# Eight seven-product slots instead of six in the second half of a feed-forward down product

## The chip, the cores and the metric

The kernel runs on one core of a Trainium2 chip. TensorE (PE) multiplies, VectorE (DVE) and ScalarE (ACT) do the elementwise work, GpSimd (POOL) almost nothing, and SyncE (SP) issues nearly all the DMAs. The metric is the device time of one execution in microseconds; the kernel before takes 1433.44 us (median of three runs, 1433.04 to 1433.55).

## The reference

One decoder block over 256 tokens of width 2048, in float32. Two attention branches are gated, merged and added to the input; then comes a feed-forward part, and a last norm over each token:

```python
h2 = rmsnorm(x, ffn_norm_w[l])
up = causal_dwconv(h2 @ w_ffn_up[l], conv_w[l], conv_b[l])
a, b = jnp.split(up, 2, axis=-1)
x = x + (jax.nn.silu(a) * b) @ w_ffn_down[l]      # 256 x 5632 times 5632 x 2048
return rmsnorm(x, final_norm_w)
```

The change touches only the product with `w_ffn_down`.

## The kernel before, in words

**Split products.** Each float32 operand is kept as a high part (rounded to the type that PE multiplies in one pass) and a low part (the rest). A product of 128x128 by 128x512 is three matmuls: high by high, high by low, low by high (`mm3`). ACT makes the high part of a weight tile by a copy (L161), DVE the low part by a subtraction (L162).

**The weight stream.** Weights come from HBM in tiles of 128x1024 called raw (512 KB, `load`, L144), always four in flight or in use (`RAW_BUFS`). `part(n)` splits tile n into whi and wlo, of which there are four each, and only then asks for tile n + 4, which takes the place of one that has been read. SP issues the loads in program order, and each waits there until its place is free.

**The down product in slots.** The 2048 output columns are four groups of 512, taken as two pairs (p = 0 and 1). The 5632 rows are 22 pieces of 256. A slot is one piece against one pair of groups: two raw tiles, two blocks of 128 tokens, two of 128 rows, two of 512 columns. As eight block products this is 24 matmuls (a plain slot). `down()` lists 22 slots for each pair; the last four of the second pair are regrouped so that column group 3 is finished first. What runs in slot q + 1 is prepared while PE works on slot q.

**Seven-product slots.** In the slots that the table `SEVEN` names, the 2x2x2 block product is done with seven block products instead of eight, so 21 matmuls, by sums of blocks on both sides. The weight side's sums are made in `seven_parts` (L685 to L698): five ACT copies and nine DVE operations over the two raw tiles, in place; L687 and L698 are 128x1024 wide, the other seven DVE operations 128x512. Its results go to whi and wlo, and to the single tiles called t (t14 and t2). The last two DVE operations (L697, L698) are also the last readers of the two raw tiles. The last products of the seven use L698's result. The token side's sums, called s, are made once for each piece by `seven_sums`: one DVE operation of 128x512 and four of 128x128 in a scratch tile called room (L717 to L721), then a high and low split. They are made in the first pair and used again in the second. Four extra sums of products, e0 to e3, collect in the accumulators that the other pair of columns does not need at that time; `gathered` adds them to x2 after the last seven-product slot, in two steps of four DVE operations.

**Between and after the pairs.** After the first pair, `added` adds the first two column groups to x2 (DVE, L786) and, a slot later, takes squares for the final norm (ACT, L790, which writes into the same accumulators). In the second pair `wf`, the weights of the final norm, is loaded into the places of one set of s and of room (L829); `weighted` multiplies them in (L795), and `finish` ends one block of 128 tokens at a time (L541 to L560).

**What sets the order.** There is no scheduler: each engine runs its instructions in program order, which is the order in which `down_slots` writes them in each slot: first the preparation of the next slot, then the sums, then one step of each task that was spawned (`run_tasks`), then the products.

Of the kernel before, what the change touches and what calls it, by code (L numbers as in the profile page):

```python
# [10 lines left out]
F32R = mybir.dt.float32r  # L11
# [6 lines left out]
P = 128  # L18
# [60 lines left out]

SEVEN = ((4, 7, 10, 13, 16, 18), (3, 5, 8, 10, 13, 15))


def down():

    out = []
    for p, where in enumerate(SEVEN):
        c = 2 * p
        rest = list(range(len(where), NFB // 4 * 2))  # L90
        for i in range(NFB // 2):
            if p == 1 and i == NFB // 2 - 4:
                for d in (c, c + 1):
                    out += [(False, [(rest[j], d), (rest[j + 1], d)]) for j in (0, 2)]
                break
            k = where.index(i) if i in where else rest.pop(0)
            out.append((i in where, [(k, c), (k, c + 1)]))
    return out
# [3 lines left out]
def block(ctx: ExitStack, tc: tile.TileContext, a):  # L102
# [8 lines left out]
    px = ctx.enter_context(tc.tile_pool(name="px", bufs=1))  # L111
# [6 lines left out]
    def f32(ap):  # L118
        return ap.bitcast(F32)
# [38 lines left out]
    def split2(hi, lo, full, scale=None):  # L158

        if scale is None:  # L160
            nc.scalar.activation(hi, full, AF.Copy)  # L161
            nc.vector.tensor_sub(lo, full, f32(hi))  # L162
        else:
            nc.scalar.activation(hi, full, AF.Copy, scale=scale)
            nc.vector.scalar_tensor_tensor(lo, full, scale, f32(hi), op0=OP.mult, op1=OP.subtract)
# [6 lines left out]
    def mm3(out, ah, al, bh, bl, start, stop, **kw):  # L172
        mm(out, ah, bh, start=start, stop=False, **kw)
        mm(out, ah, bl, start=False, stop=False, **kw)
        mm(out, al, bh, start=False, stop=stop, **kw)
# [71 lines left out]
    xb = [xtiles[k // 2][:, k % 2] for k in range(KD)]  # L247
# [7 lines left out]
    big = {}  # L255
# [447 lines left out]
    def two_blocks(k):  # L703

        f = 2 * k
        if f < 16:
            x = "rm"[f // 8]
            return ot[x + "h"][:, f % 8:f % 8 + 2, :], ot[x + "l"][:, f % 8:f % 8 + 2, :]
        return big["gh"][:, f - 16:f - 14, :], big["gl"][:, f - 16:f - 14, :]

    def seven_sums(k):


        ah, al = two_blocks(k)
        room = big["room"]
        x, sums = room[:, 0, :].rearrange("p (k t) -> p k t", k=2), room[:, 1, :].rearrange("p (i t) -> p i t", i=4)
        nc.vector.tensor_add(x, f32(ah), f32(al))  # L717
        nc.vector.tensor_add(sums[:, 0, :], x[:, 0, P:], x[:, 1, P:])
        nc.vector.tensor_sub(sums[:, 2, :], x[:, 0, :P], x[:, 0, P:])
        nc.vector.tensor_sub(sums[:, 1, :], sums[:, 0, :], x[:, 0, :P])  # L720
        nc.vector.tensor_sub(sums[:, 3, :], x[:, 1, :P], sums[:, 1, :])  # L721
        pool_k, tag = (px, f"xb{k}") if k < 5 else (big["pf"], "wa")
        big["s", k] = pool_k.tile([P, 2, 4, P], F32R, name=f"s{k}", tag=tag, bufs=1)
        split2(big["s", k][:, 0], big["s", k][:, 1], sums)

    def seven_products(k, accs, extra, halves):

        xs = two_blocks(k)
        sums = big["s", k]

        def a(t, kk):
            return [x[:, kk, t * P:(t + 1) * P] for x in xs]

        def b(half, kk):
            return [x[:, kk * CW:(kk + 1) * CW] for x in halves[half]]

        ss = [[sums[:, x, i, :] for x in range(2)] for i in range(4)]
        t1, t4 = [[x[:, i * CW:(i + 1) * CW] for x in big["t14"]] for i in range(2)]
        t2 = [big["t2"][:, x, :] for x in range(2)]
        for key, (ah, al), (bh, bl) in (  # L740
                ("e0", a(0, 0), b(0, 0)), ((0, 0), a(0, 1), b(0, 1)), ((0, 1), ss[3], b(1, 1)),
                ("e3", ss[2], b(1, 0)), ("e2", ss[1], t2), ("e1", ss[0], t1), ((1, 0), a(1, 1), t4)):
            begin, end = accs.edges(key, 3)
            mm3(accs.bank(key), ah, al, bh, bl, begin, end, to=stream)
# [52 lines left out]
    def down_slots(slot):  # L797

        slots = down()
        per = len(slots) // 2  # L800
        tiles = [[ps.tile([P, 2, 512], F32, name="acc", bufs=2), second_pair()], None]
        for i, (seven, where) in enumerate(slots):
            p, q = divmod(i, per)
            if p == 0 and q == 3:
                tiles[1] = [ps.tile([P, 2, 512], F32, name="acc", bufs=2), second_pair()]
            if q == 0:
                counts = {}
                for sv, at in slots[p * per:(p + 1) * per - 2 * p]:
                    keys = [(0, 0), (0, 1), (1, 0), "e0", "e1", "e2", "e3"] if sv else [
                        (t, d - 2 * p) for _, d in at for t in range(NT) for _ in range(2)]  # L810
                    for key in keys:
                        counts[key] = counts.get(key, 0) + 3
                at = Banks(2 * p, tiles[0] if p == 0 else tiles[1], tiles[1] if p == 0 else tiles[0], counts)
            at.main, at.extra = (tiles[0], tiles[1]) if p == 0 else (tiles[1], tiles[0])
            n = 2 * (slot + 1)
            if i + 1 < len(slots):
                if slots[i + 1][0]:
                    seven_parts(n)
                else:
                    part(n)  # L820
                    part(n + 1)
            if p == 0 and q in (1,) + SEVEN[0][:-1]:
                seven_sums(((1,) + SEVEN[0]).index(q))
            if q == SEVEN[p][-1] + 1:
                spawn(gathered, at)
            if p == 1 and q == SEVEN[1][-1] + 1:
                big["wf"] = [big["pf"].tile([P, 2 * CW], F32, name="wf", tag=x, bufs=1) for x in ("wa", "wb")]
                for j, wf in enumerate(big["wf"]):
                    nc.sync.dma_start(wf, a["wf"][None, 2 * CW * j:2 * CW * (j + 1)].to_broadcast([P, 2 * CW]))  # L829
            if p == 1 and q == per - 4:  # L830
                spawn(added, at.main[1], 3, False)
            if p == 1 and q == per - 3:
                weighted(0, 2)
            if p == 1 and q == per - 2:
                spawn(added, at.main[0], 2)
            run_tasks()
            if p == 1 and q == per - 1:
                weighted(2, 1)
            halves = [parts.pop(2 * slot + h) for h in range(2)]
            if seven:  # L840
                seven_products(where[0][0], at, None, halves)
                issue()
            elif p == 1 and q >= per - 2:
                if q == per - 2:
                    held = list(zip(where, halves))
                else:
                    held += zip(where, halves)
                    for t in range(NT):
                        acc = at.extra[t][:, 0, :]
                        for h, ((k, d), (hi, lo)) in enumerate(held):  # L850
                            for j in range(2):
                                x = [y[:, j, t * P:(t + 1) * P] for y in two_blocks(k)]
                                w = slice(j * CW, (j + 1) * CW)
                                mm3(acc, *x, hi[:, w], lo[:, w], h + j == 0, h == 3 and j == 1, to=stream)
                        issue()
                        finish(acc, t)
            else:
                for (k, d), (hi, lo) in zip(where, halves):
                    xs = two_blocks(k)
                    for j in range(2):  # L860
                        w = slice(j * CW, (j + 1) * CW)
                        for t in range(NT):
                            key = (t, d - 2 * p)
                            begin, end = at.edges(key, 3)
                            mm3(at.bank(key), *(x[:, j, t * P:(t + 1) * P] for x in xs), hi[:, w], lo[:, w],
                                begin, end, to=stream)
                issue()
            slot += 1
            if p == 0 and q == per - 1:
                assert not tasks, len(tasks)  # L870
                for d in range(2):
                    spawn(added, at.main[d], d)
# [131 lines left out]
```

## Time and profile before

| | |
|---|---|
| median of 3 runs | 1433.44 us |
| the profiled execution | 1433.27 us, its span 1431.5 us |
| PE busy | 1420.8 us, 99% of the span |
| DVE busy | 977.0 us, 68% |
| ACT busy | 743.0 us, 52% |
| weight loads | 503 DMAs, nearly all of 512 KB, 4.1 us median to landing |
| granted TensorE clock | 0.999 mean |

A matmul's listed duration is longer than its share of PE's time, since matmuls overlap; the pace is read from starts. "x2" in a row of the timeline stands for two instructions in a row. The second product runs from about 1196 us to the end, its second pair of column groups from 1307 us.

### The profile page before, as it was taken

Reading aid. Unit: us, or ns where it says so; the run is one execution under the profiler, and the core shown is the slowest. Engines: PE = TensorE matmul, PEld = TensorE weight load, DVE = VectorE, ACT = ScalarE, POOL = GpSimd, SP = SyncE. Lnnn points to the kernel's source line nnn. Section 1 sums busy time; section 2 is a strip of 40 time slices with the busy share of each in tenths; the row PEclk is TensorE's granted clock in tenths of the full one; section 3 lists DMA queues with packets and bytes.
Section 4 is the critical chain, followed back from the end, with each engine's and each line's share of the span. In section 5 each row is a group of like instructions: output and inputs, shape, how many; then the busy total and the mean of one; then the engine's idle time right before and its main releaser. Section 6 shows DMA issues by size and latency. Waiting matters only on the chain. (4 is left out here: it accounts for less than half of the span.)

```text
span 1431.5 us, 19274 instructions
## 1 busy us (share of the span) xinstructions
PE 1420.8 (99%) x7354; PEld 1218.1 (85%) x7354; DVE 977.0 (68%) x1294; ACT 743.0 (52%) x1004; POOL 6.4 (0%) x14
## 2 busy tenths in 40 slices
PE   9999999999999999999999999999999999999997
PEld 7888888888888888888998888888888888888886
DVE  6687656657554545455567777777777778998777
ACT  6545454544544444444455555555555555555553
POOL 0000000000000000000000000000000000000000
PEclk9999999999999999999999999999999999999999
DMA  8755565555666666666655656565555655656664
GB/s 298 265 177 166 159 193 167 187 177 185 181 190 192 191 191 190 197 215 202 190 183 188 195 181 197 182 195 188 189 193 182 197 181 167 206 186 206 206 210 172
DMA packets 77836, 276.22 MB, mean 193 GB/s; under 512 B 8720, under 2 KB 10288, under 8 KB 77744
## 3 DMA queue, kind: packets, MB, share of 16 engines
q1 hardware_dynamic: 77312, 274.27, 60.1%
q8 instruction: 57, 0.93, 0.3%
q10 hardware_dynamic: 432, 0.73, 0.1%
q14 instruction: 35, 0.29, 0.1%
HBM read 272.86 MB, written 2.10 MB: 192 GB/s over the span
## 5 line engine op out<-in xcount | busy, mean ns | idle before, releaser
L162 DVE TENSOR_TENSOR wlo<-raw,whi 128x1024 fp32r<-128x1024 f32 (+1 forms) x481 | 574.3, 1220 | 386.4 <-ACT whi L161 252.1
L161 ACT ACTIVATE whi<-raw 128x1024 fp32r<-128x1024 f32 (+1 forms) x481 | 502.6, 1056 | 515.3 <-PE acc L170 370.7
L170 PE MATMUL acc<-xb,whi 128*128 128x512 f32 (+1 forms) x1984 | 473.3, 385 | 1.0 <-ACT whi L161 1.0
L170 PEld LDWEIGHTS acc<-xb,whi 128*128 128x128 f32 x1984 | 359.2, 189 | 66.4 <-ACT whi L161 2.0
L170 PE MATMUL acc<-whi,xb 128*128 128x512 f32 x896 | 282.1, 391 | 0.0
L170 PEld LDWEIGHTS acc<-xb,wlo 128*128 128x128 f32 x1920 | 254.4, 191 | 11.6
L170 PE MATMUL acc<-xb,wlo 128*128 128x256 f32 x1920 | 263.8, 283 | 0.0
L170 PEld LDWEIGHTS acc<-whi,xb 128*128 128x128 f32 x896 | 168.3, 188 | 34.5
L170 PE MATMUL acc<-wlo,xb 128*128 128x512 f32 x448 | 174.6, 390 | 0.0
L170 PEld LDWEIGHTS acc<-wlo,xb 128*128 128x128 f32 x448 | 84.2, 188 | 16.6
L170 PE MATMUL acc<-wlo,gh 128*128 128x512 f32 x224 | 87.4, 390 | 0.2 <-DVE wlo L162 0.2
L170 PE MATMUL acc<-whi,gh 128*128 128x512 f32 x224 | 87.2, 389 | 0.0
L170 PE MATMUL acc<-whi,gl 128*128 128x512 f32 x224 | 87.2, 389 | 0.0
L525 DVE SCALAR_TENSOR_TENSOR y<-u,vec,y 128x256 f32<-128x256 f32 x176 | 73.5, 483 | 0.0
L170 PEld LDWEIGHTS acc<-wlo,gh 128*128 128x128 f32 x224 | 42.0, 188 | 9.8 <-DVE wlo L162 1.1
L170 PE MATMUL acc<-whi,mgh 128*128 128x512 f32 x128 | 50.1, 392 | 0.0
L170 PE MATMUL acc<-whi,mgl 128*128 128x512 f32 x128 | 49.8, 389 | 0.0
L170 PE MATMUL acc<-wlo,mgh 128*128 128x512 f32 x128 | 49.8, 389 | 0.0
L170 PEld LDWEIGHTS acc<-whi,gh 128*128 128x128 f32 x224 | 42.1, 188 | 8.7
L170 PEld LDWEIGHTS acc<-whi,gl 128*128 128x128 f32 x224 | 42.0, 188 | 8.7
L522 ACT ACTIVATE y<-u,vec 128x256 f32<-128x256 f32 x88 | 47.6, 588 | 0.0
L170 PE MATMUL acc<-whi,otmh 128*128 128x512 f32 x104 | 40.6, 390 | 0.0
(207 smaller groups left out, 1165.7 us busy)
## 6 DMA issues: line engine op xcount, KB each, us to landing
raw<-in_wts SPq DMA_DIRECT2D x503, 512.0 KB, 4.1
rows<-in_x SPq DMA_DIRECT2D x4, 512.0 KB, 7.6
xp<-in_x SPq DMA_DIRECT2D x4, 512.0 KB, 5.5
xt<-in_xT SPq DMA_DIRECT2D x3, 512.0 KB, 6.7
out<-x SPq DMA_DIRECT2D x6, 224.0 KB, 3.1
wf<-in_wf SPq DMA_DIRECT2D x2, 512.0 KB, 7.5
out<-x ACTq DMA_DIRECT2D x2, 352.0 KB, 3.1
xt<-in_xT SPq DMA_DIRECT2D x2, 256.0 KB, 4.4
```

The source lines that it names most:

```text
L161: nc.scalar.activation(hi, full, AF.Copy)
L162: nc.vector.tensor_sub(lo, full, f32(hi))
L170: to.append(lambda: nc.tensor.matmul(out, a, b, **kw))
L522: nc.scalar.activation(y[:, j, :], u[:, j, 0:S], AF.Identity, scale=cv[j][:, 0:1], bias=cv[j][:, 3:4])
L525: nc.vector.scalar_tensor_tensor(y[:, j, :], u[:, j, i:i + S], cv[j][:, i:i + 1], y[:, j, :], op0=OP.mult, op1=OP.add)
```

## The change

The table for the second pair names eight slots, every other one from 2 to 16, instead of six. So the second pair uses eight pieces' token sums where there were six, and `seven_sums` is called twice more: for piece 6 in the first pair's last slot and for piece 7 in the second pair's slot 2. The sums of pieces 6 and 7 lie in the places of u0 and u1 and of the two y tiles, which the feed-forward's first product used; a set is now a pair of tiles, high and low, not one tile. Because the last seven-product slot is 16 and not 15, the gathering and wf's load come one slot later.

```diff
-SEVEN = ((4, 7, 10, 13, 16, 18), (3, 5, 8, 10, 13, 15))
+SEVEN = ((4, 7, 10, 13, 16, 18), (2, 4, 6, 8, 10, 12, 14, 16))
...
-        pool_k, tag = (px, f"xb{k}") if k < 5 else (big["pf"], "wa")
-        big["s", k] = pool_k.tile([P, 2, 4, P], F32R, name=f"s{k}", tag=tag, bufs=1)
-        split2(big["s", k][:, 0], big["s", k][:, 1], sums)
+        if k < 6:
+            pool_k, tag = (px, f"xb{k}") if k < 5 else (big["pf"], "wa")
+            both = pool_k.tile([P, 2, 4, P], F32R, name=f"s{k}", tag=tag, bufs=1)
+            big["s", k] = [both[:, 0], both[:, 1]]
+        else:
+            tags = (("u0", 1), ("u1", 1)) if k == 6 else (("y", 2), ("y", 2))
+            big["s", k] = [big["pf"].tile([P, 4, P], F32R, name=f"s{k}{i}", tag=tag, bufs=n)
+                           for i, (tag, n) in enumerate(tags)]
+        split2(*big["s", k], sums)
...
-        ss = [[sums[:, x, i, :] for x in range(2)] for i in range(4)]
+        ss = [[x[:, i, :] for x in sums] for i in range(4)]
...
                 seven_sums(((1,) + SEVEN[0]).index(q))
+            if (p, q) in ((0, per - 1), (1, 2)):
+                seven_sums(6 + p)
             if q == SEVEN[p][-1] + 1:
                 spawn(gathered, at)
```

Lines behind L721 stand six to eight further down in the changed file: `added` is L786 and L790 before, L792 and L796 after.

Three places show what it moves. First DVE from the end of the first pair to the first seven-product preparation of the second. Before (L162 on whi and raw are weight halves; L786 the two additions of the first pair; L687 begins a preparation):

```order
L781 TENSOR_TENSOR x_5238<-acc,x_5238 128x512
L162 TENSOR_TENSOR wlo<-raw,whi 128x1024 x4
L786 TENSOR_TENSOR x_5238<-acc,x_5238 128x2x512
L786 TENSOR_TENSOR x_5238<-acc_10396,x_5238 128x2x512
L162 TENSOR_TENSOR wlo<-raw,whi 128x1024 x2
L687 TENSOR_TENSOR wlo<-raw,whi 128x1024
```

After:

```order
L787 TENSOR_TENSOR x_5238<-acc,x_5238 128x512
L162 TENSOR_TENSOR wlo<-raw,whi 128x1024 x2
L717 TENSOR_TENSOR room<-otmh,otml 128x512
L718 TENSOR_TENSOR room<-room 128x128
L719 TENSOR_TENSOR room<-room 128x128
L720 TENSOR_TENSOR room<-room 128x128
L721 TENSOR_TENSOR room<-room 128x128
L162 TENSOR_TENSOR s_11308<-room,s_11307 128x512
L162 TENSOR_TENSOR wlo<-raw,whi 128x1024 x2
L792 TENSOR_TENSOR x_5238<-acc,x_5238 128x2x512
L792 TENSOR_TENSOR x_5238<-acc_10396,x_5238 128x2x512
L687 TENSOR_TENSOR wlo<-raw,whi 128x1024
```

The set of sums for piece 6 stands between slot 0's and slot 1's weight halves, and the preparation follows the additions at once, without slot 2's halves ahead of it.

Second ACT at the same place, up to the second preparation. Before (L685 begins a preparation; the two rows of L790 are the four squares):

```order
L161 ACTIVATE whi<-raw 128x1024 x8
L790 ACTIVATE acc,ss_5240<-x_5238 128x512 x2
L790 ACTIVATE acc_10396,ss_5240<-x_5238 128x512 x2
L685 ACTIVATE whi<-raw 128x1024
L686 ACTIVATE whi<-raw 128x512
L691 ACTIVATE whi<-raw 128x512
L693 ACTIVATE t_10393<-raw 128x512
L695 ACTIVATE t_10391<-raw 128x1024
L161 ACTIVATE whi<-raw 128x1024 x2
L685 ACTIVATE whi<-raw 128x1024
```

After:

```order
L161 ACTIVATE s_11307<-room 128x512
L161 ACTIVATE whi<-raw 128x1024 x2
L685 ACTIVATE whi<-raw 128x1024
L686 ACTIVATE whi<-raw 128x512
L691 ACTIVATE whi<-raw 128x512
L693 ACTIVATE t_10393<-raw 128x512
L695 ACTIVATE t_10391<-raw 128x1024
L796 ACTIVATE acc,ss_5240<-x_5238 128x512 x2
L796 ACTIVATE acc_10396,ss_5240<-x_5238 128x512 x2
L161 ACTIVATE whi<-raw 128x1024 x2
L161 ACTIVATE s_11440<-room 128x512
L685 ACTIVATE whi<-raw 128x1024
```

The squares have gone from ahead of the first preparation to behind it, and the copies for slot 3 and for piece 7's sums stand behind them.

Third DVE after the last preparation (L773 and L778 begin the two steps of the gathering, L795 is the weighting). Before:

```order
L162 TENSOR_TENSOR wlo<-raw,whi 128x1024 x4
L773 TENSOR_TENSOR x_5238<-acc,x_5238 128x512
L774 TENSOR_TENSOR y<-acc,y 128x512
L775 TENSOR_TENSOR x_5238<-x_5238,y 128x512
L776 TENSOR_TENSOR x_5238<-acc,x_5238 128x512
L162 TENSOR_TENSOR wlo<-raw,whi 128x1024 x2
L778 TENSOR_TENSOR y<-acc_10396,y 128x512
```

After, the rows read the same, but the last preparation is slot 16's: the four halves are those of slots 17 and 18 and not of 16 and 17, and one plain slot fewer is left behind the gathering.

## Rows read from the trace of the kernel before

**Rows 1.** Windows: stretch, its us, busy us (instructions) by engine, clock, DMA, GB/s.
```profile
1300.00:1400.00 100.00, 100.00 (x443) 82.71 (x442) 80.82 (x92) 53.84 (x66) 0.00 (x0) 1.00 0.63 204
```
**Rows 2.** Waits, 1200 to 1432 us: us in total, times, longest.
```profile
PEld acc L170 <- DVE t L698: 0.4, 1, 0.4
```
**Rows 3.** Timeline of PE: start, us, instruction; first matmuls of slots 0 and 15.
```profile
1307.33 0.39 PE L170 MATMUL acc<-whi,otmh 128*128 128x512 f32 x1
...
1385.53 0.39 PE L170 MATMUL acc<-whi,otmh 128*128 128x512 f32 x1
```
**Rows 4.** Timeline of DVE, preparations of slots 3, 5, 13, 15; idle before in brackets.
```profile
1323.67 1.23 DVE L698 TENSOR_TENSOR t<-raw,t 128x1024 fp32r<-128x1024 f32 x1
...
1334.93 1.23 DVE L698 TENSOR_TENSOR t<-raw,t 128x1024 fp32r<-128x1024 f32 x1
...
1370.48 1.23 DVE L687 TENSOR_TENSOR wlo<-raw,whi 128x1024 fp32r<-128x1024 f32 x1 [0.50 <-ACT whi L685]
...
1376.22 1.23 DVE L698 TENSOR_TENSOR t<-raw,t 128x1024 fp32r<-128x1024 f32 x1
...
1380.93 1.23 DVE L687 TENSOR_TENSOR wlo<-raw,whi 128x1024 fp32r<-128x1024 f32 x1 [1.21 <-ACT whi L685]
1382.79 0.69 DVE L688 TENSOR_TENSOR wlo<-raw,whi 128x512 fp32r<-128x512 f32 x1 [0.63 <-ACT whi L686]
...
1387.47 1.22 DVE L698 TENSOR_TENSOR t<-raw,t 128x1024 fp32r<-128x1024 f32 x1
```
**Rows 5.** Timeline of ACT, start of slot 15's preparation.
```profile
1379.84 1.06 ACT L685 ACTIVATE whi<-raw 128x1024 fp32r<-128x1024 f32 x1 [1.75 <-DMA raw<-in_wts]
1382.12 0.63 ACT L686 ACTIVATE whi<-raw 128x512 fp32r<-128x512 f32 x1 [1.22 <-DMA raw<-in_wts]
```
**Rows 6.** Tile raw, SP's issues at 1376.3 and 1377.5: time to landing of each.
```profile
DMA to landing us min/median/max: 3.4/3.4/3.4
...
DMA to landing us min/median/max: 4.5/4.5/4.5
```
**Rows 7.** Timeline of DVE, then of ACT, start of the second pair.
```profile
1304.33 3.49 DVE L162 TENSOR_TENSOR wlo<-raw,whi 128x1024 fp32r<-128x1024 f32 x3
...
1309.76 2.35 DVE L786 TENSOR_TENSOR x<-acc,x 128x1024 f32<-128x1024 f32 x2
...
1313.93 0.58 ACT L790 ACTIVATE acc<-x 128x512 f32<-128x512 f32 x1
...
1316.67 1.04 ACT L685 ACTIVATE whi<-raw 128x1024 fp32r<-128x1024 f32 x1
```
**Rows 8.** Timeline of DVE, first pair: sums between the preparations of slots 16 and 18.
```profile
1275.85 1.23 DVE L698 TENSOR_TENSOR t<-raw,t 128x1024 fp32r<-128x1024 f32 x1
...
1279.26 0.68 DVE L717 TENSOR_TENSOR room<-otmh,otml 128x512 f32<-128x512 f32 x1
...
1282.65 1.22 DVE L687 TENSOR_TENSOR wlo<-raw,whi 128x1024 fp32r<-128x1024 f32 x1 [0.26 <-ACT whi L685]
...
1288.46 1.22 DVE L698 TENSOR_TENSOR t<-raw,t 128x1024 fp32r<-128x1024 f32 x1
```
**Rows 9.** Timeline of DVE, from the gathering to the end.
```profile
1395.35 0.68 DVE L773 TENSOR_TENSOR x<-acc,x 128x512 f32<-128x512 f32 x1
...
1398.00 2.35 DVE L162 TENSOR_TENSOR wlo<-raw,whi 128x1024 fp32r<-128x1024 f32 x2
...
1409.16 2.29 DVE L795 TENSOR_TENSOR x<-x,wf 128x2048 f32<-128x2048 f32 x1
...
1413.45 1.23 DVE L162 TENSOR_TENSOR wlo<-raw,whi 128x1024 fp32r<-128x1024 f32 x1 [0.87 <-ACT whi L161]
...
1423.23 0.76 DVE L545 TENSOR_TENSOR x<-acc,x 128x256 f32<-128x256 f32 x2 [0.46 <-PE acc L170]
```
**Rows 10.** Windows as in rows 1, after PE's last matmul.
```profile
1427.00:1428.00 1.00, 0.00 (x0) 0.00 (x0) 0.01 (x1) 0.00 (x0) 0.00 (x0) 1.00 0.89 325
1428.00:1430.00 2.00, 0.00 (x0) 0.00 (x0) 0.00 (x0) 0.00 (x0) 0.00 (x0) 0.53 0.97 362
```

## The prediction

> **What bounds the kernel now.** I read the busy time by stretch first. Over the stage that holds the second pair of column groups, PE is busy 100.00 of 100 us at clock 1.00, VectorE (DVE) 80.82 and ScalarE (ACT) 53.84 [rows 1]. TensorE is the bound there, and DVE is the engine with the least room. The waits came next: in the whole second product PE's loads wait for an L698 result once, for 0.4 us [rows 2]. That one wait is the warning. The timeline then gives the pace: from the first matmul of slot 0 (1307.33) to that of slot 15 (1385.53) lie five slots of 21 matmuls and ten of 24, 345 in 78.20 us, 0.2267 us each [rows 3]. So a plain slot is 5.44 us, a seven-product slot 4.76, and a seven and a plain one together 10.20.
>
> The preparation of a seven (L685 to L698) is not that fast. Its 13th and 15th slots are such a pair. DVE prepares one from 1370.48 to 1376.22 + 1.23 = 1377.45, which is 6.97 us; two plain halves follow (2.35 in [rows 9]) until 1379.7; then it stands idle for ACT, starts the next seven at 1380.93, idles again until 1382.79, and ends at 1388.69 [rows 4]. ACT in turn waits for the two weight tiles [rows 5]. The reason is the ring of four raw tiles: the loads for the next seven go out only when this seven's L697 and L698 have freed theirs, and they land 3.4 and 4.5 us later [rows 6]. From one L698 end to the next it is 11.24 us here, 11.26 in the pair 3 and 5 (1323.67 to 1334.93) [rows 4]. Call it 11.25: two sevens with one plain slot between them are prepared 1.05 us slower than PE uses them up.
>
> What pays for that today is lead. The L698 result is read by the slot's 17th matmul, 3.63 us after its first, and that one's weights a matmul earlier: due 3.4 us after the first. For slot 13 (first matmul one pair, 10.20, before that of slot 15: 1375.33) it was there after 2.12 us, for slot 15 after 3.16 [rows 3, 4]: the lead fell from 1.28 to 0.24 us. The two plain slots that follow each such pair rebuild it (5, then 8; 10, then 13). The change takes these away.
>
> **The change, part by part.** *Matmuls.* Two more sevens remove 2 x 3 x 0.2267 = 1.36 us of PE time.
>
> *The way in.* The first seven moves from slot 3 to slot 2, and both new sets of sums (L717 to L721 and a split) stand ahead of the second seven on DVE. Before, DVE does three plain halves from 1304.33, so slot 0's two are done at 1306.6 [rows 7]. The first new sums go in here. A set holds DVE until the next instruction for 3.39 us where a preparation follows (1279.26 to 1282.65, of which 0.26 is a wait for ACT) [rows 8], so some 3.1: 1309.7. Slot 1's halves follow, now behind ACT, which had to wait for the sums (its copies end at about 1310.05 and 1311.0): 1312.4. The two additions (2.35, the tail of which overlaps) end at 1314.7; then the seven's 6.97: L698 ends at 1321.7. Slot 2's first matmul would be at 1307.33 + 2 x 5.44 = 1318.21, due 1321.6. Just in time, with no lead.
>
> Behind it on ACT now stand the four squares of the first pair (before they stood ahead of the preparation): 1313.93 to 1316.67, 2.74 us [rows 7]. ACT reaches them 5.7 us into the preparation, at 1320.4, and ends at 1323.1. Two things wait there. The squares write into the very accumulators that the seven's four extra sums take, so slot 2 itself starts up to 3 us late. And slot 3's copies come behind them, 1323.1 to 1325.1, their subtractions to 1326.5; then the second new sums, 3.4, to 1329.9; then the seven, 7.03 in the like place (1282.65 to 1288.46 + 1.22) [rows 8]: L698 for slot 4 ends at 1336.9. PE without a stall would want it at 1318.21 + 10.20 + 3.4 = 1331.8. PE loses 5.1 us by there, and the earlier late start of slot 2 is inside that, not on top.
>
> *The long run.* From slot 4 to slot 16 come six more pairs with nothing between. The four loads of one cycle have landed long before the next cycle's go out, so each should repeat the measured cycle: 6 x (11.25 - 10.20) = 6.3 us. PE's lateness gives the loop nothing back: the buffers that it frees are free well before the loads land. A cycle is bounded from below by DVE's own work, 6.97 + 2.3 = 9.3 us (then there is no stall), and from above by the one pair that has a set of sums between its sevens, 1275.85 to 1288.46 or 12.6 us [rows 8], a loss of 2.4. I take 1.05, because the two pairs of this very order give it.
>
> The DMA page of the Trainium skill (DMA: Bandwidth & Descriptors, "Measured") gives 6.15 us for 1 MB from HBM on another queue. The two tiles here need 5.7 us from the first issue to the second landing [rows 6]. By the page a cycle would be some 0.45 us longer and the whole about 2.7 us more, as an estimate; the rows have the queue in question, and I stay with them.
>
> *The way out.* Before, after the last seven DVE has two pairs of halves (the second waits for loads) until 1395.35, which is 6.66 us after 1388.69, then gathers 2.65, and so on [rows 4, 9]. After, the gathering is one slot nearer the end, and wf's load and the gathering follow slot 16. From L698's end: 6.66 + 2.65 (gather) + 2.3 (halves) + 2.65 (gather) + 1.2 (addition) + 2.3 (halves) + 2.2 (weighting) = 19.9; slot 21's first half is split at 21.1. PE starts slot 17 at +1.4 (4.76 less 3.4), its last group at 1.4 + 3 x 5.44 = 17.7, and needs that half after 12 more matmuls: 20.4. It stalls 0.7. And the last rows: from the last half (1413.45) to the second row block's addition DVE needs 1423.23 - 1413.45 = 9.8, of which 0.46 is a wait for PE [rows 9]; after: 21.05 + 9.3 = 30.4, against a PE end at 1.4 + 27.2 + 0.7 = 29.3. Together 1.8 us that PE's cover hid before. Bounds: 0 (DVE faster through the waits), 3 (both wf tiles or the last raw tiles late).
>
> *At nothing.* The other storage: both tiles of u and of y are free by then (the last FFN block and the first pair's gather), and the second gather takes y when slot 16 has read its sums, 5 us before DVE comes to it. wf leaves one slot later and lands before the weighting at about +17.7, as long as it needs no more than 10 us. The two sums' own time is in the way in.
>
> Sum: -1.36 + 5.1 + 6.3 + 1.8 = +11.8 us. The profiled execution took 1433.27 us (span 1431.5), so 1445.1; the median of 1433.44 is 0.17 above it. I say 1445.
>
> **Rivals.** *No stall, only fewer matmuls*: 1433.3 - 1.4 = 1432. For it: PE shows no stall in six sevens. Against: the lead is down to 0.24 at slot 15, and nothing rebuilds it. It decides the other way only if a cycle is at most 10.20, a load landing 1 us sooner. 7%.
>
> *The way in costs, the run keeps pace*: -1.4 + 5.1, and some way out: 1437 to 1438. For it: with steady alternation the loads might meet a quieter queue. Against: two pairs agree within 0.02. 8%.
>
> *The run costs, the way in doesn't* (ACT takes the copies in time): -1.4 + 7 x 1.05 + 1.8 less what lead there is: 1440 to 1441. Against: the order of ACT's instructions. 11%.
>
> *The clock falls at each stall.* Matmuls at 1.2 GHz take 0.453 us; the five left in a seven and the plain slot behind it would cost 29 x 0.2267 = 6.6 us, less the 1.05 of the stall that they make unnecessary; seven times, up to 39 us: 1484. Against: with no matmul after 1423.2 [rows 9] the granted clock reads 1.00 still in 1427 to 1428 and 0.53 only in the next stretch [rows 10], and my stalls are 1 to 3 us. 3%. TensorE: Matmul & The Clock Gate ("HAM oscillation") of the Trainium skill tells of just such a kernel, whose matmul groups alternate with waits for loads and run throttled each time; by that rule this rival would lead; the row at the end, and stalls of this size, speak against it so far.
>
> **How the numbers follow.** The forecast has 68%, with its own range 1442 to 1448 (way in and out 1.5 either way, cycles 0.1 each). Another 3% is for what is longer than that without the clock. 1437 to 1449 takes in the two smaller losses and leaves out the first rival, the clock and the rest. A measurement can tell about 0.2%, 2.9 us: slower is all but the first rival, 0.93; the first rival lies within it at 0.05, and beyond it at 0.02 (faster), where the sevens' shorter slots give more than counted.
>
> **What would show it.** Right: in the second pair PE waits at every seven from slot 4 on for DVE's L698 or L697, about 1 us each; L698 repeats every 11.2 us; ACT L685 and L686 wait for DMA in each cycle; slot 2's first matmul waits for ACT (the squares); the first L698 ends near 1321.7, the second near 1337; PE busy in 1340 to 1400 is near 91%. Wrong: L698 every 10.2 us with PE at 100%, the second L698 before 1333, or a granted clock under 1.00 in the stage.

## The result, and the profile after

The changed kernel takes 1445.78 us (median of five runs, 1444.10 to 1446.09) against 1433.44 (five runs, 1433.04 to 1433.64): 1.0081 times the time before, with a 95% interval of 1.0069 to 1.0092. That is 12.3 us slower; 1445 had been forecast, in a range of 1437 to 1449. The profiled execution took 1445.93 us, 12.66 more than that of before, and all steps below are read against these 12.66.

The windows of after come first (stretch, its us, busy us and instructions of PE, PEld, DVE, ACT and POOL, granted clock, DMA share, GB/s); the first line answers to [rows 1]:

```profile
1300.00:1400.00 100.00, 94.28 (x397) 74.61 (x396) 83.06 (x104) 50.21 (x65) 0.00 (x0) 0.98 0.54 180
...
1321.00:1322.00 1.00, 0.09 (x1) 0.09 (x1) 0.75 (x1) 0.97 (x4) 0.00 (x0) 1.00 0.65 70
1322.00:1323.00 1.00, 1.00 (x3) 0.81 (x4) 0.00 (x0) 0.97 (x3) 0.00 (x0) 0.55 0.73 266
1323.00:1324.00 1.00, 1.00 (x3) 0.79 (x3) 0.00 (x0) 1.00 (x3) 0.00 (x0) 0.50 0.92 344
1324.00:1325.00 1.00, 1.00 (x4) 0.73 (x3) 0.80 (x1) 1.00 (x2) 0.00 (x0) 0.50 0.80 324
1325.00:1326.00 1.00, 1.00 (x5) 0.81 (x4) 1.00 (x2) 0.12 (x1) 0.00 (x0) 0.75 0.13 53
1326.00:1327.00 1.00, 1.00 (x6) 0.83 (x5) 1.00 (x2) 0.00 (x0) 0.00 (x0) 1.00 0.70 94
...
1340.00:1400.00 60.00, 57.71 (x244) 44.83 (x243) 48.69 (x58) 30.63 (x37) 0.00 (x0) 1.00 0.57 195
```

PE is no longer busy throughout: 94.28 of 100 us, and 397 matmuls where before had 443. The busy share hides a part of the loss, because a matmul is listed as 0.39 us long although the next can start after 0.2267. In 1340 to 1400 the busy share is 96%, but 244 matmuls at 0.2267 us are 55.3 us, 92% of the stretch. For an engine that pipelines, count the starts.

The waits of after, from 1200 us to the end (us in total, times, longest), which answer to [rows 2]:

```profile
ACT whi L685 <- DMA raw<-in_wts: 11.3, 7, 2.1
...
ACT whi L686 <- DMA raw<-in_wts: 7.3, 6, 1.7
...
PEld acc L170 <- DVE wlo L696: 4.2, 5, 1.1
PEld acc L170 <- DVE t L698: 4.0, 7, 0.6
...
PE acc L170 <- ACT acc L796: 3.4, 1, 3.4
...
PE acc L170 <- DVE wlo L162: 1.4, 2, 1.2
```

PEld is PE's weight load, and its waits overlap those of PE. Where before had a single 0.4 us for a seven, beside 1.1 us in two waits for weight halves, three kinds stand here: one long wait for the squares (L796), a short one for L696 or L698 in the sevens, and one for a weight half (L162) near the end. The timeline of PE gives their places (start, us, instruction, idle before); its slots 2 and 4 begin with the otrh rows at 1321.91 and 1333.85, slot 17 with the row at 1406.21, and the last row is the kernel's last matmul:

```profile
1318.10 0.39 PE L170 MATMUL acc<-whi,gl 128*128 128x512 f32 x1
1321.91 0.66 PE L170 MATMUL acc<-whi,otrh 128*128 128x512 f32 x1 [3.43 <-ACT acc L796]
1322.37 0.63 PE L170 MATMUL acc<-wlo,otrh 128*128 128x512 f32 x1
...
1333.85 0.39 PE L170 MATMUL acc<-whi,otrh 128*128 128x512 f32 x1
...
1403.13 0.50 PE L170 MATMUL acc<-wlo,s 128*128 128x512 f32 x1 [0.63 <-DVE wlo L696]
...
1404.96 0.73 PE L170 MATMUL acc<-t,s 128*128 128x512 f32 x2 [0.18 <-DVE t L698]
...
1406.21 0.39 PE L170 MATMUL acc<-whi,gh 128*128 128x512 f32 x1
...
1426.80 0.50 PE L170 MATMUL acc<-wlo,gh 128*128 128x512 f32 x1 [1.16 <-DVE wlo L162]
...
1434.64 0.39 PE L170 MATMUL acc<-whi,gl 128*128 128x512 f32 x1
```

These starts divide the 12.66 us:

| part | how it is read | us | forecast |
|---|---|---|---|
| matmuls | 6 fewer at 0.2267 | -1.36 | -1.36 |
| way in | slot 2 was due 0.23 after 1318.10; slot 4 one pair later, at 1328.53, and starts at 1333.85 | +5.3 | +5.1 |
| long run | slot 4 to slot 17: 72.36, at pace 6 x 10.20 + 4.76 = 65.96 | +6.4 | +6.3 |
| way out | the rest: PE +1.4 up to its last matmul, +0.8 behind it | +2.3 | +1.8 |

DVE shows why (answering to [rows 4] and the last row of [rows 9]; L698 of slots 2, 4, 6 and 16, the start of slot 6's preparation, the end):

```profile
1320.53 1.23 DVE L698 TENSOR_TENSOR t<-raw,t 128x1024 fp32r<-128x1024 f32 x1
...
1335.67 1.23 DVE L698 TENSOR_TENSOR t<-raw,t 128x1024 fp32r<-128x1024 f32 x1
...
1340.45 1.23 DVE L687 TENSOR_TENSOR wlo<-raw,whi 128x1024 fp32r<-128x1024 f32 x1 [1.29 <-ACT whi L685]
...
1346.73 1.23 DVE L698 TENSOR_TENSOR t<-raw,t 128x1024 fp32r<-128x1024 f32 x1
...
1403.68 1.23 DVE L698 TENSOR_TENSOR t<-raw,t 128x1024 fp32r<-128x1024 f32 x1
...
1435.90 0.74 DVE L545 TENSOR_TENSOR x<-acc,x 128x256 f32<-128x256 f32 x2
```

From slot 4's L698 to slot 16's lie six cycles and 68.01 us, 11.34 each (10.96 to 11.63); PE needs 10.20. The last addition no longer waits for PE, as it did by 0.46 us in [rows 9]: the chain of DVE and ACT ends the kernel. ACT's timeline shows what DVE waits for (answering to [rows 5, 7]):

```profile
1320.40 0.58 ACT L796 ACTIVATE acc<-x 128x512 f32<-128x512 f32 x1
...
1323.13 1.99 ACT L161 ACTIVATE whi<-raw 128x1024 fp32r<-128x1024 f32 x2
...
1339.36 1.06 ACT L685 ACTIVATE whi<-raw 128x1024 fp32r<-128x1024 f32 x1 [1.83 <-DMA raw<-in_wts]
1341.39 0.63 ACT L686 ACTIVATE whi<-raw 128x512 fp32r<-128x512 f32 x1 [0.97 <-DMA raw<-in_wts]
```

In every cycle ACT waits for the two weight tiles that could be asked for only when the last preparation had read theirs, and slot 3's copies stand behind the squares.

### The profile page after: what moved, and what is told of

It reads as the page before. It is cut to its first block, busy times and chain, and to the rows that moved or that the text cites. A ratio compares the mean times of both kernels' runs of the same rounds, so it can differ in the third digit from the quotient of the medians.

```text
span 1444.1 us, 19306 instructions
## 1 busy us (share of the span) xinstructions
PE 1424.8 (99%) x7348; PEld 1217.0 (84%) x7348; DVE 990.0 (69%) x1320; ACT 747.1 (52%) x1012; POOL 6.4 (0%) x14
## 5 line engine op out<-in xcount | busy, mean ns | idle before, releaser
L162 DVE TENSOR_TENSOR wlo<-raw,whi 128x1024 fp32r<-128x1024 f32 (+1 forms) x477 | 568.9, 1220 | 383.0 <-ACT whi L161 248.5
L170 PE MATMUL acc<-whi,otmh 128*128 128x512 f32 x92 | 35.9, 390 | 0.0
```

The source lines that it names most:

```text
L170: to.append(lambda: nc.tensor.matmul(out, a, b, **kw))
```

## The experiments

Two theories were open. One is the forecast's: the loop is late because four raw tiles let a seven's loads go out only at the end of the preparation before. Its rival: DVE has too much to do for a seven in every second slot. A second question was what sets the way in. Line numbers differ by up to three between these kernels; each row keeps its own. Runs e1 to e4 were made beside before at 1433.66 us, e5 to e8 on another chip beside before at 1433.92.

**e1_ring5: a fifth raw tile.** Room for it was made by moving sums into u and y, and wf into the tiles of used-up sums; slot 14 multiplies with piece 5's sums, in as many instructions.

```diff
-RAW_BUFS, PART_BUFS = 4, 4
+RAW_BUFS, PART_BUFS = 5, 4
...
+    for i in range(4, RAW_BUFS):
+        load(i)
```

> The changed kernel with five raw weight tiles instead of four. To make room, piece 5's sums lie in u0 and u1, both new sets are written to the two y tiles one after the other, and slot 14 multiplies with piece 5's sums in place of piece 6's (so that slot's result is left wrong; instructions and their number are the same). Theory (the cycle of two sevens is long because their loads leave only when L697 and L698 have freed the ring): L685 finds its tile there, L698 follows L698 after at most 10.3 us, PE runs without stalls from slot 6 on, the 6.8 us of the long run and about 1 us of the way out are gone: 1438 us (1436.5 to 1439.5). Rival (DVE's own work is too long for two slots): no change, 1445 to 1446.5, with L698 still every 11.3 us.

Measured: 1436.9 us (1436.46 to 1438.07), ratio 1.0022 [1.0013, 1.0032]. The window of the long run, and two L698 in a row (here L700), with the start of the preparation between them:

```profile
1340.00:1400.00 60.00, 60.00 (x265) 49.53 (x264) 56.75 (x68) 36.80 (x44) 0.00 (x0) 1.00 0.68 225
```

```profile
1354.47 1.22 DVE L700 TENSOR_TENSOR t<-raw,t 128x1024 fp32r<-128x1024 f32 x1
...
1357.89 1.22 DVE L689 TENSOR_TENSOR wlo<-raw,whi 128x1024 fp32r<-128x1024 f32 x1
...
1363.69 1.23 DVE L700 TENSOR_TENSOR t<-raw,t 128x1024 fp32r<-128x1024 f32 x1
```

PE is busy for all 60 us, and a cycle is 9.2 us where DVE has to catch up, without an idle time in it: the forecast had worked out 9.3 us as DVE's own work. So DVE could keep up all along. The rival falls. PE's starts (first matmuls of slots 2, 5 and 17) show that slots 5 to 16 take 61.46 us, where six pairs at pace take 61.20:

```profile
1322.08 0.50 PE L170 MATMUL acc<-whi,otrh 128*128 128x512 f32 x1 [1.29 <-ACT acc L797]
...
1338.39 0.39 PE L170 MATMUL acc<-whi,gh 128*128 128x512 f32 x1
...
1399.85 0.39 PE L170 MATMUL acc<-whi,gh 128*128 128x512 f32 x1
```

**e2_store4: the same storage, four raw tiles**, the control for e1. It lacks the two edits shown for e1 and is otherwise the same kernel.

> The control for the five tiles: the same storage of the sums and of wf, and the same wrong sums in slot 14, with four raw tiles. Theory and rival both: as the changed kernel, 1445.8 us within 1.2. If it is much faster, the storage and not the ring made the difference.

Measured: 1445.15 us (1444.79 to 1446.77), ratio 1.0082 [1.0066, 1.0099], as after. Two L698 (of slots 4 and 16), then PE's first matmuls of slots 5 and 17 and its longest wait behind them:

```profile
1335.57 1.23 DVE L698 TENSOR_TENSOR t<-raw,t 128x1024 fp32r<-128x1024 f32 x1
...
1401.82 1.23 DVE L698 TENSOR_TENSOR t<-raw,t 128x1024 fp32r<-128x1024 f32 x1
```

```profile
1339.58 0.39 PE L170 MATMUL acc<-whi,gh 128*128 128x512 f32 x1
...
1404.35 0.39 PE L170 MATMUL acc<-whi,gh 128*128 128x512 f32 x1
...
1426.22 0.50 PE L170 MATMUL acc<-wlo,gh 128*128 128x512 f32 x1 [1.41 <-DVE wlo L162]
```

The six cycles between the two take 66.25 us, 11.04 each. The fifth tile alone is worth 1445.15 - 1436.9 = 8.2 us. Of the 8.1 us between the two profiled executions (spans 1443.6 and 1435.5 us) 1.2 had come by slot 5, 3.3 come from slot 5 to slot 17 and 3.6 behind it, at the end that DVE then reaches in time. The way in is hardly shorter: slot 2 starts no sooner in e1 than in after (1322.08, 1321.91), and its wait is 1.3 us instead of 3.4 only because PE comes to it 2.3 us later, by a loss in the opening (see e3). This answers to a passage of the Trainium skill (Perfetto Trace Analysis, "Identifying Performance Opportunities"): the same gap repeating on the engine that should be saturated can mean that there is no room for the next tile. The gap of about 1 us in each cycle was of that kind, and these two runs price it.

**e3_before_ring5: a fifth raw tile in before.**

```diff
-RAW_BUFS, PART_BUFS = 4, 4
+RAW_BUFS, PART_BUFS = 5, 4
```

> The kernel before with five raw tiles (piece 5's sums in u0 and u1, wf in the places of two used-up sets); its result is the full one. Theory: PE is the bound there and has no stall to give back, so 1433.4 within 0.7. Rival (loads are late everywhere): 2 us or more faster.

Measured: 1435.28 us (1434.93 to 1436.9), ratio 1.0014 [1.0004, 1.0023]. That it gains nothing in before's second pair was right; that it costs nothing was not: 1.6 us. The timelines of ACT and of PE show where:

```profile
18.49 1.06 ACT L161 ACTIVATE whi<-raw 128x1024 fp32r<-128x1024 f32 x1 [4.15 <-DMA raw<-in_wts]
...
19.59 2.11 PE L170 MATMUL acc<-xb,whi 128*128 128x512 f32 x8 [1.66 <-ACT whi L161]
```

In the opening, ACT waits 4.15 us for a weight tile, and PE 1.66 us for its high half. PE's next product starts at 30.87 us and not at 29.27 as before: that is the whole 1.6. The edit's own order explains it. `part` now asks for tile n + 5, so tiles 5 and 6 are asked for before the new loop asks for tile 4; the load that ACT waits for is issued at 10.5 us, where before issued tile 4's at 7.5. The order was not tried apart, but in e7, where the fifth place is first used from tile 60 on, that product starts at 29.60. e1 has the same order and loses 2.3 us there; its total doesn't show it, because slot 2 waits for the squares that much less.

**e4_squares_y: the first pair's squares written elsewhere**, so that slot 2 doesn't wait for the accumulators; ACT's order is as in after.

```diff
-                nc.scalar.activation(acc[:, t, :], x3[:, t, :], AF.Square, accum_out=big["ss3"][:, t, c:c + 1])
+                to = acc[:, t, :] if c > 1 else big["pf"].tile([P, CW], F32, name="sq", tag="y", bufs=2)
+                nc.scalar.activation(to, x3[:, t, :], AF.Square, accum_out=big["ss3"][:, t, c:c + 1])
```

> The changed kernel, with the four squares of the first pair written to y tiles and not into the accumulators, so that slot 2 has nothing to wait for there. Theory of the prediction (the second preparation ends at 1336.9 whatever slot 2 does): slot 2 starts on time at about 1318.3 and the granted clock stays 1.00, but PE then waits for slot 3's halves (2 us) and for slot 4's L698, still near 1336.9; in all 1445.5, at most 1 us under the changed kernel. Rival (what costs in the way in is the 3.4 us wait for the accumulators and the half clock behind it, some 5 us): 1440 to 1441.

Measured: 1445.91 us (1445.74 to 1446.01), ratio 1.0085 [1.007, 1.01]. The longest wait of after, 3.4 us, is gone, and nothing is won. PE's waits in slots 3 and 4:

```profile
1323.43 0.50 PE L170 MATMUL acc<-whi,gh 128*128 128x512 f32 x1 [0.61 <-ACT whi L161]
1324.69 0.50 PE L170 MATMUL acc<-wlo,gh 128*128 128x512 f32 x1 [0.76 <-DVE wlo L162]
1333.01 0.50 PE L170 MATMUL acc<-whi,s 128*128 128x512 f32 x1 [0.46 <-ACT whi L691]
1334.40 0.50 PE L170 MATMUL acc<-wlo,s 128*128 128x512 f32 x1 [0.89 <-DVE wlo L696]
```

The clock is 1.00 in each stretch, yet slot 4's L698 still ends only at 1334.93 + 1.22 = 1336.15, 0.75 us before that of after: it hangs on ACT and DVE. Two paths of about equal length led to slot 4 in after, and one of them was enough. The 1.15 us by which PE starts slot 5 sooner (1337.46, in after 1338.61) are lost again by the end, where PE waits for a weight half as late as in after (1426.80):

```profile
1426.82 0.50 PE L170 MATMUL acc<-wlo,gh 128*128 128x512 f32 x1 [1.42 <-DVE wlo L162]
```

**e5_no_sums: the two new sets of sums not made.**

```diff
-            if (p, q) in ((0, per - 1), (1, 2)):
-                seven_sums(6 + p)
...
-        sums = big["s", k]
+        sums = big["s", k if k < 6 else k - 6]
```

> The changed kernel without the two new sets of sums: slots 14 and 16 multiply with pieces 0's and 1's sums (so these two slots' result is left wrong). The four raw tiles and the eight slots stay. Theory (one PE time line, pushed back by whatever of the preparations ends last): the first preparation begins 3 us sooner, the squares end near 1320, slot 2 waits under 1 us and the clock stays 1.00; the second L698 ends near 1330 and not 1337, so the way in costs 0.5 and not 5 us and leaves some 2 us of lead; the six cycles of 11.3 then cost 5; in all 1439.7 us (1438.5 to 1441). L698 repeats as slowly as in the changed kernel. Rival (the sums run in DVE's idle time and only the cycles cost): 1445 or more.

Measured: 1441.17 us (1440.24 to 1441.39), ratio 1.0049 [1.0036, 1.0063]: by the two ratios 4.6 us less than after, and just above the upper end expected, 1441. The first two L698:

```profile
1318.32 1.22 DVE L698 TENSOR_TENSOR t<-raw,t 128x1024 fp32r<-128x1024 f32 x1
1330.07 1.23 DVE L698 TENSOR_TENSOR t<-raw,t 128x1024 fp32r<-128x1024 f32 x1
```

They stand 2.2 and 5.6 us before those of after; the six cycles behind them take 67.17 us, 11.20 each. So the sums cost time only through the way in, and the cycles are about as long without them. PE's wait for the last half:

```profile
1421.11 0.50 PE L170 MATMUL acc<-wlo,gh 128*128 128x512 f32 x1 [1.46 <-DVE wlo L162]
```

**e6_seven7: slot 16 plain again, both new sets still made.**

```diff
-SEVEN = ((4, 7, 10, 13, 16, 18), (2, 4, 6, 8, 10, 12, 14, 16))
+SEVEN = ((4, 7, 10, 13, 16, 18), (2, 4, 6, 8, 10, 12, 14))
```

> The changed kernel without its last seven-product slot: 2, 4, ... 14; both sets of sums are still made, piece 7's is not used; the gathering and wf's load stand two slots earlier. Theory: one cycle less (-1.1), three more matmuls (+0.7), and the 2 us that the way out cost come back, since two more plain slots of PE lie over DVE's last work: 1443.2 us (1442.3 to 1444.3). Rival (the way out costs nothing, the rest is all in the cycles and the way in): 1445.4.

Measured: 1442.57 us (1442.46 to 1443.68), ratio 1.0063 [1.0048, 1.0078]. The last addition:

```profile
1432.41 0.75 DVE L545 TENSOR_TENSOR x<-acc,x 128x256 f32<-128x256 f32 x2 [0.46 <-PE acc L170]
```

It waits for PE by 0.46 us, as in before: with seven plain slots behind the last seven-product slot, where after has five and before has six, the way out is hidden again. By the two ratios the eighth seven costs 2.6 us of after's 12.3.

**e7_best12 and e8_best8: all eight sevens, with what the runs had shown.** Five raw tiles, the fifth asked for only from tile 60 on; the squares into room, one at a time in four slots; piece 7's sums made in slot 12 (e8: slot 8) instead of slot 2.

```diff
+                if n <= 60:
+                    load(n + 4)
+                if n >= 60:
+                    load(n + 5)
...
-            if (p, q) in ((0, per - 1), (1, 2)):
+            if (p, q) in ((0, per - 1), (1, 12)):
```

> Eight seven-product slots at 2, 4, ... 16 with each loss taken out: five raw tiles (the fifth is asked for only from tile 60 on, so that the opening is as before), the four squares one at a time at slots 2, 4, 6, 8, written to room and not into the accumulators, piece 7's sums made at slot 12 in the place of set 0, wf in the places of sets 1 and 2; the result is the full one. Theory: L698 of slot 2 is just in time, of slot 4 at about 1332 (0 to 0.5 late), every later one early; PE loses under 1 us and saves 1.36: 1432.6 us (1431.8 to 1433.6), at or just under the kernel before. Rival (DVE is too full for eight sevens whatever the loads do): 1436 or more.

> The same with piece 7's sums made at slot 8. Theory: DVE's lead is some 1.8 us smaller there than at slot 12 when the sums take 3.4 us of it, so a stall of up to 1 us at slot 10: 1432.6 to 1433.6 us, equal to the run with slot 12 or up to 1 us slower. Rival (DVE too full): 1436 or more.

Measured: e7 1432.24 us (1432.16 to 1432.69, 11 runs), ratio 0.9988 [0.9979, 0.9997]; e8 1433.27 us (1432.85 to 1433.6), 0.9994 [0.9986, 1.0003]. The long run of e7:

```profile
1340.00:1400.00 60.00, 60.00 (x265) 49.53 (x265) 55.45 (x69) 34.92 (x45) 0.00 (x0) 1.00 0.65 219
```

and in e8 the first matmuls of slots 10 and 11:

```profile
1359.56 0.39 PE L173 MATMUL acc<-whi,otmh 128*128 128x512 f32 x1
...
1365.34 0.39 PE L173 MATMUL acc<-whi,gh 128*128 128x512 f32 x1
```

Eight sevens can be fed: e7 gains 1.7 us on the before of its chip (by its interval 0.4 to 3.0), against 1.36 worked out from the matmuls; e8 can't be told from before. e7's L698 (L701 there) have a gap of 13.4 us where the sums go in, after five cycles of 9.4 to 10.5 had built a lead; in e8, four slots earlier, the lead is smaller and does not quite carry it. Slot 10 takes 5.78 us there instead of 4.76, which is the 1.0 us between e7 and e8; PE's listed waits in it are only 0.3 and 0.2 us.

## Why the prediction was right

*What bounds.* Right: the pace of PE, the due time of L698 and the thin lead are what decides. The rival without a stall falls with the first wait.

*The way in.* The sum was right (5.1, measured 5.3), and so were DVE's and ACT's times: L698 of slot 2 ended at 1321.76 (1321.7 said), that of slot 4 at 1336.90 (1336.9), the squares ran from 1320.40 to 1323.1 (1320.4 to 1323.1). The mechanism was right only in part. The forecast had the late accumulators as contained in the late L698. In the trace slot 2 waited 3.43 us, and then its matmuls started 0.43 us apart, at a granted clock of 0.50, until 1325. By the starts, the wait cost PE 1321.91 - 1318.33 = 3.6 us and the low clock the other 1.7 of the 5.3, so PE itself came to slot 4 at 1333.85, and L698 at 1336.90 was just in time for the due time of 1333.85 + 3.4. e4 takes the wait and the low clock away, and the other path gives the same total. The forecast's sum was safe because it took the longer of two paths, but the step that it named was, in this execution, not the one that PE waited for. PE's first stall for a seven's own weights is therefore in slot 6, and not in slot 4 as forecast.

*The long run.* Right in size and cause: 6.4 us for 6.3. Cycles of 11.34 us on average, six times, lose 6.8, of which the 0.35 us that L698 was early at slot 4 covers a part. e1 and e2 show the cause, late loads behind four tiles; e5 shows that the sums have no part in it. That each part of the table came out so near its forecast is in part luck. By the same starts e2 divides its 12.1 us into 6.3 for the way in (its clock was low for longer), 3.6 for the long run and 3.6 for the way out, and the total is the same. What repeats, within 1.3 us, is the chain of loads, ACT and DVE: from the end of slot 4's L698 to the matmul that waits for the last half it takes 89.9 us in after, 89.4 in e2, 90.7 in e4 and 89.8 in e5. The forecast's terms make 6 x 11.25 + 21.1 = 88.6 of it. PE's waits only say where PE meets this chain. One signpost was off: PE busy "near 91%" was counted from starts, and the busy share that the page prints reads 96%. And the wait for L696 (0.63 us at slot 16) came ahead of that for L698 (0.18): when the whole preparation is late, the first of its results that PE wants stalls it, and the later ones find part of the delay taken already.

*The way out.* 1.8 said, 2.3 by the table. The stall for the half of the last slots is 1.16 us (0.7 said); the second row block's addition starts at 1435.90, 31.0 us after the last L698 ended (30.4 said), without waiting for PE. Plain slots behind the last seven hide it (before six, e6 seven), and so does a DVE that comes in time: in e1, with five as in after, the last addition again waits 0.46 us for PE. At nothing stood the storage, and e2 agrees: with the sums elsewhere, the time is the same.

*The clock.* One of the forecast's own signs of being wrong did come, a granted clock under 1.00 in the stage (0.98 in 1300 to 1400). This rival was half right: the clock fell in one place, behind the one long wait, and not behind those of about 1 us; it cost 1.7 us and not 39, and even that was hidden. A matmul took 0.43 us there, 0.453 was said. The Trainium skill (TensorE: Matmul & The Clock Gate, "HAM oscillation") tells of a kernel that waits after each group of matmuls for longer than the group lasts, and whose groups all run throttled. The one wait of 3.43 us here, with the low clock behind it, agrees with that. The long run, with some 10 us of work and about 1 us of stall in each of six cycles at clock 1.00, is no such case, and the forecast read the section too widely when it let it lead this rival.

*The rest.* What remains open is the size of the cycles: 10.96 to 11.63 us in one execution, when the loads of a cycle landed sooner or later, and 11.04 on average in e2 against 11.34 in after. What is left in e1 is the way in: slot 5 was due at 1333.17 (1318.21 and, for slots 2 to 4, 14.96) and starts at 1338.39, 5.2 us late (after: 5.4); with 0.3 us behind it and -1.4 for the matmuls that makes 4.1, and the span is 4.0 us longer than that of before.

## What to carry to other kernels

A saving on a saturated engine is worth its size only as long as what feeds it keeps pace: compare the period of the preparation with that of the use, and look for the slots in which lead is rebuilt before you take them away. Where a load reuses the tile that is being read, the period is the preparation plus the landing, not the work of the busiest engine; one more tile took 8.2 us off here, and a busy share of 81% on the feeding engine said nothing of it. When two late chains end at the same place, taking one away shows next to nothing, as e4 did.

## What the runs showed of the hardware

TensorE's clock fell from 1.00 to 0.50 (from 2.4 to 1.2 GHz) after PE had stood 3.43 us, and in after the low clock came only with the first matmuls behind the wait: the stretch 1321 to 1322 still reads 1.00, 1323 to 1325 0.50, 1326 to 1327 1.00 again. In e2 and e6 a wait of 3.4 and 3.3 us was followed by the low clock too, but not for the same time: in e2 it read 0.50 from 1321 to 1327, already ahead of the first matmul at 1321.82, in e6 from 1322 to 1324 (0.66 and 0.83 on average over 1320 to 1330). In e1 and e5, where the wait was 1.3 and 1.2 us, the clock stayed at 1.00. The length of a wait alone doesn't tell it, though: at the end of before the clock read 1.00 for almost 5 us after the last matmul [rows 10]. Nor does it decide the time here: four of after's five executions have a mean clock of 0.997, the fifth has 0.999, as the profiled one of before, and took 1446.09 us, the longest of the five.
